# TensorE's order in the first attention written by hand, and identity products ahead of the first weights

## The chip, the cores and the metric

The kernel runs on one core of a Trainium2 chip. The metric is the device time of one execution in microseconds (us), lower is better. A core has a matrix engine (TensorE, "PE" in the profile, with its weight loads as "PEld"), a vector engine (VectorE, "DVE"), an engine for activation functions (ScalarE, "ACT"), a general engine (GpSimd, "POOL") and a sync engine (SyncE, "SP"), which here issues the loads. TensorE writes to PSUM, in banks of 128 x 512 float32; the other engines read it from there. Every engine takes its own instructions strictly in order, and waits for other engines on semaphores.

## What is computed

Two layers over 256 tokens of width 1024, in float32. Layer 0 is a differential attention with 8 heads and a mixer of product-key experts; layer 1 a stick-breaking attention and the same mixer; each sub-layer ends in a layer norm of `alpha * x + f(x)`. The edit touches the first attention:

```python
qkv = x @ w_qkv
q, k, v = qkv[..., :D], qkv[..., D:2 * D], qkv[..., 2 * D:]
q, k = _rope(q), _rope(k)                       # per head of 64
s = einsum('bhmqd,bhmkd->bhmqk', q, k) * scale  # m: two score maps per head
p = softmax(where(mask, s, -inf))
a = p[:, :, 0] - lam * p[:, :, 1]
o = einsum('bhqk,bhkd->bhqd', a, v)
of = o * rsqrt(mean(o * o) + RMS_EPS) * subln_g * (1 - lambda_init)
return of @ w_o
```

The mask is causal in chunks of 64, so the first 128 queries see 128 keys and the second 128 see 256.

## The kernel before

Products with weights are made in three parts. A weight chunk is loaded raw by SyncE; ScalarE copies its upper half to `h` (L144), and VectorE or GpSimd subtracts to get the lower half `l` (L149); `Units.split` alternates the two engines by the parity of `self.n` for units of kind "a". `passes` (L196) then accumulates `xh h`, `xh l` and `xl h`. The raw, `h` and `l` tiles come from a pool of three buffers each. A unit is 128 x 1024.

`diff_attention` (L375) runs in this order of writing:

- The Q projection in eight steps (`moving_steps`, L212), one unit each, four PSUM banks of tag "acc"; `x_in` loads and splits x between the first steps.
- The K projection in eight steps, into the four banks of tag "w". Meanwhile `rope_half` (L386) rotates Q in four pieces, one per token block `b` and half `f` of the columns: VectorE L393, L394 and L395 from PSUM, then an addition on GpSimd (L396). `tr` (L398) transposes the rotated Q on TensorE (L404) in four pairs of 128 columns, and ScalarE (L406) and VectorE (L407) split each into upper and lower half.
- The V projection in eight V steps (`v_steps`, L435) of twelve 512-wide products (L444), with two evacuations (L448) after the fourth and the eighth. K is rotated and transposed as Q was.
- Per group of two heads, `s1(i)`: 64-row score products (L465), b = 1 256 wide and b = 0 128 wide, the mask product (L468), the maximum (VectorE L470), the exponentials (ScalarE L473), the combination of the two maps (L475, L476, L482). `s2(i)`: six transposes (L493) and two ScalarE copies (L494). `s3(i)`: value products (L504, L506), square (ScalarE L516), sum and scaling (VectorE L517 to L520), a power on GpSimd (L521), L522 and L523. `s4(i)`: four transposes (L532) and the split of the attention's output (L533, L534).
- The output projection `wo`, `moving_steps` over eight units (L199), of which the last three go through `tail_passes`; the units of the next projection are loaded and split behind it (`prefetch`, GpSimd L173). Then the layer norm (transposes L312) and the expert mixer's query projection (L244).

PSUM tags "acc" and "w" have four banks each, and scores, transposes and the key projection share "w". A scheduler puts the instructions of each engine in order, by its own estimate of when their inputs are there, except where `tc.manual_schedule` names an engine: there its instructions keep the order in which the code is written. Before, that holds for TensorE in `tail_passes`.

Of the kernel before, what the change touches and what calls it, by code (L numbers as in the profile page):

```python
# [10 lines left out]
F32 = mybir.dt.float32  # L11
# [9 lines left out]
P = 128  # L21
D = 1024
T = 256
NB = 2
# [9 lines left out]
EPS = 1e-5  # L34
GS = 2.0 ** 14
OH = 5

SPANS = []
_o = 0
# [19 lines left out]
def trunk(ctx: ExitStack, tc: tile.TileContext, x, xT, ln_g, ln_b, w_qkv, w_o_a, lam_p, subln, w_kv,  # L59
          w_q, w_o_b, w_pq, sub_k, uT, v, rope, ln_c, out):  # L60
    nc = tc.nc
# [57 lines left out]

    class Units:  # L120
        def __init__(self):
            self.n = 0

        def get_cut(self, src):
            self.n += 1
# [249 lines left out]
    def diff_attention(xh, xl):  # L375
# [19 lines left out]
            nc.vector.tensor_tensor(dv, pv, cs, OP.mult)  # L395
            nc.gpsimd.tensor_tensor(dv, dv, tv, OP.add)  # L396

        def tr(srcv, dstT, tag):  # L398
            for i in range(4):
                pt = psum.tile([P, 2, T], F32, name=tag, tag=tag)  # L400
                for j in range(2):
                    for b in range(NB):
                        n = 2 * i + j
                        nc.tensor.transpose(pt[:, j, b * P:(b + 1) * P], srcv[:, b, n * P:(n + 1) * P], ident)  # L404
                h, l = (t[i] for t in dstT)
                nc.scalar.activation(h, pt, AF.Copy)  # L406
                nc.vector.tensor_tensor(l, pt, h.bitcast(F32), OP.subtract)  # L407
# [6 lines left out]

        halves = [(b, f) for b in range(NB) for f in range(2)]
        aq = accs("acc")
        x_in(0)
        for d, _ in enumerate(moving_steps(aq, xh, xl, src(0), cut=True)):
            if d < 3:
# [3 lines left out]
        ak = accs("w")  # L423
# [110 lines left out]
            nc.vector.scalar_tensor_tensor(ol[:, hs, :], pt, sg, oh[:, hs, :].bitcast(F32), OP.mult, OP.subtract)  # L534

        av = accs("acc")
        for i, _ in enumerate(v_steps(av)):
            if 1 <= i < 5:
                rope_half(ak, KK, *halves[i - 1], 2)
            if i == 4:  # L540
                tr(KK, KT, "w")
                s1(0)
            if i == 5:
                s1(1)
                s2(0)
                s3(0)
            if i == 6:
                s1(2)
                s1(3)
            if i == 7:  # L550
                s2(1)
                s3(1)
        units.later(reg(O_A, NB, D), x)
        oh, ol = xtiles()
        acc = accs("acc")
        wo = moving_steps(acc, oh, ol, lambda d: w_o_a[0, d * P:(d + 1) * P, :], tail=TAIL,
                          ahead=(pq_src(0), range(0, 4096, 1024)))
        for i in range(4):
            if i < 2:
                s2(i + 2)  # L560
                s3(i + 2)
            s4(i, oh, ol)
            next(wo)
            next(wo)
        for _ in wo:
            pass
        return acc
# [516 lines left out]
```

## Time and profile before

| | |
|---|---|
| runs | 1888.84, 1892.78, 1894.35 us |
| median | 1892.78 us |
| profiled execution | 1894.14 us |
| its span, first to last instruction | 1892.3 us |
| TensorE busy | 1831.4 us (97%) |
| granted TensorE clock, mean over the span | 0.989 |

The first attention takes about the first 138 of the 1892 us. TensorE starts at 5.12, the K projection at 31.03, the V projection at 55.63; the next projection's first product stands at 138.22. In a row of the trace the first number is the start, the second the time the instruction took; "x12" says that twelve alike were joined; brackets give the idle time of the engine before it and the engine, tile and line that ended it. Durations of neighbouring products overlap, so the work of a step is read from the starts.

### The profile page before, as it was taken

What the parts mean: (1) busy time and instruction counts of PE and PEld (TensorE: products, weight loads), DVE (VectorE), ACT (ScalarE), POOL (GpSimd) and SP (SyncE); (2) the same over time, 40 slices, a digit from 0 to 9 for tenths busy, and PEclk for the clock granted to TensorE, in tenths of its full rate; (3) what the DMA queues carried; (4) which work ended last, traced back from release to release, by engine and by line L of the source; (5) the groups of instructions that cost most, each with busy time, mean ns of one, the idle gap of its engine ahead of it and who ended that gap; (6) DMA issues with size and microseconds to landing.
All of it is one profiled execution on the core that took longest, in us unless ns stands there. A gap on an engine that the chain in (4) does not pass through costs nothing.

```text
span 1892.3 us, 30931 instructions
## 1 busy us (share of the span) xinstructions
PE 1831.4 (97%) x12264; PEld 1655.8 (87%) x12264; DVE 1232.2 (65%) x2402; ACT 911.5 (48%) x1244; POOL 176.6 (9%) x190
## 2 busy tenths in 40 slices
PE   8999989999999999999999999899999999999997
PEld 6879989898999999978798799889989999998786
DVE  5666988986555555575553569889865555555655
ACT  4545445545444444454447454454544444445442
POOL 5434200000000000000122251000000000000001
PEclk9989999999999999999999999999999999999999
DMA  6533544335555555575643345443355555555753
GB/s 210 177 134 135 184 136 137 123 124 200 179 200 191 191 186 182 186 266 190 211 152 105 123 157 179 133 146 113 134 202 184 191 181 189 185 191 192 255 190 133
DMA packets 90449, 325.40 MB, mean 172 GB/s; under 512 B 10176, under 2 KB 10560, under 8 KB 89664
## 3 DMA queue, kind: packets, MB, share of 16 engines
q1 hardware_dynamic: 90304, 323.43, 50.4%
q8 instruction: 96, 1.57, 0.3%
q14 instruction: 49, 0.40, 0.1%
HBM read 320.24 MB, written 3.15 MB: 171 GB/s over the span
## 4 chain that ended last, share of the span: by engine, by line
PE 77%; DVE 17%; DMA 2%; issue 2%; ACT 1%; POOL 1%; SPq 0%; POOLq 0%; ACTq 0%; DVEq 0%
PE acc L199 38%; PE w L816 28%; PE acc L244 4%; DVE l L149 3%; DVE gl L900 2%; DVE big L873 2%; DVE gh L900 2%; DVE oa L904 1%; PE w L244 1%; PE acc L444 1%; PE w L199 1%; DVE big L707 1%; DVE big L709 1%; DMA big<-in_ln_g 1%; DVE big L714 1%
## 5 line engine op out<-in xcount | busy, mean ns | idle before, releaser
L144 ACT ACTIVATE h<-raw 128x1024 fp32r<-128x1024 f32 x579 | 606.9, 1059 | 854.7 <-PE acc L199 457.0
L149 DVE TENSOR_TENSOR l<-raw,h 128x1024 fp32r<-128x1024 f32 x526 | 642.8, 1235 | 530.4 <-ACT h L144 530.1
L816 PE MATMUL w<-xh,l 128*128 128x256 f32 x2048 | 580.3, 285 | 15.6 <-DVE l L149 15.6
L816 PE MATMUL w<-xh,h 128*128 128x256 f32 x2048 | 586.6, 287 | 2.1 <-ACT h L144 2.1
L816 PE MATMUL w<-xl,h 128*128 128x256 f32 x2048 | 580.6, 284 | 0.0
L816 PEld LDWEIGHTS w<-xh,l 128*128 128x128 f32 x2048 | 392.8, 192 | 21.6 <-DVE l L149 16.6
L199 PE MATMUL acc<-l,wh 128*128 128x512 f32 x1024 | 399.3, 391 | 2.9 <-DVE l L149 2.9
L816 PEld LDWEIGHTS w<-xh,h 128*128 128x128 f32 x2048 | 393.8, 192 | 7.9 <-ACT h L144 2.5
L199 PE MATMUL acc<-h,wl 128*128 128x512 f32 x1024 | 399.5, 391 | 0.0
L816 PEld LDWEIGHTS w<-xl,h 128*128 128x128 f32 x2048 | 393.7, 192 | 4.8
L199 PE MATMUL acc<-h,wh 128*128 128x512 f32 x1024 | 278.3, 391 | 0.0
L199 PEld LDWEIGHTS acc<-l,wh 128*128 128x128 f32 x1024 | 192.6, 188 | 40.0 <-DVE l L149 3.8
L199 PEld LDWEIGHTS acc<-h,wl 128*128 128x128 f32 x1024 | 192.8, 188 | 36.8
L199 PEld LDWEIGHTS acc<-h,wh 128*128 128x128 f32 x1024 | 188.1, 188 | 35.6
L149 POOL TENSOR_TENSOR l<-raw,h 128x1024 fp32r<-128x1024 f32 x53 | 130.4, 2461 | 178.2 <-ACT h L144 167.4
L959 DVE TENSOR_TENSOR wl<-big,wh 128x512 fp32r<-128x512 f32 x128 | 87.0, 687 | 5.1 <-PE acc L199 4.7
L173 POOL TENSOR_TENSOR ahead<-big,ahead 128x512 fp32r<-128x512 f32 x12 | 16.5, 1403 | 754.2 <-ACT ahead L163 754.2
L958 ACT ACTIVATE wh<-big 128x512 fp32r<-128x512 f32 x128 | 78.2, 620 | 12.1 <-PE acc L199 7.8
L915 PE MATMUL acc<-oa,gl 128*128 128x128 f16 x512 | 66.3, 220 | 14.2 <-DVE gl L900 12.7
L295 POOL TENSOR_TENSOR mv<-mv,mhalf 128x1 f32<-128x1 f32 x8 | 4.8, 600 | 745.1 <-DVE mv L294 745.1
L914 PE MATMUL acc<-oa,gh 128*128 128x128 f16 x512 | 70.6, 220 | 0.0
L874 ACT ACTIVATE big<-acc 128x344 f32<-128x344 f32 x128 | 51.4, 453 | 30.5 <-DVE big L873 30.5
(215 smaller groups left out, 1749.2 us busy)
## 6 DMA issues: line engine op xcount, KB each, us to landing
raw<-in_uT SPq DMA_DIRECT2D x256, 512.0 KB, 3.3
raw<-in_v SPq DMA_DIRECT2D x256, 512.0 KB, 3.6
raw<-in_w_qkv SPq DMA_DIRECT2D x23, 512.0 KB, 3.7
raw<-in_w_kv SPq DMA_DIRECT2D x12, 512.0 KB, 4.0
raw<-in_w_o_a SPq DMA_DIRECT2D x8, 512.0 KB, 4.0
big<-in_w_pq SPq DMA_DIRECT2D x8, 512.0 KB, 6.7
raw<-in_w_pq SPq DMA_DIRECT2D x8, 512.0 KB, 5.0
raw<-in_w_q SPq DMA_DIRECT2D x8, 512.0 KB, 3.8
```

Of the source, the lines that this page charges most:

```text
L144: self.h = nc.scalar.activation(h, raw, AF.Copy)
L149: o = e.tensor_tensor(l, raw, h.bitcast(F32), OP.subtract)
L199: nc.tensor.matmul(acc[b][f], a[:, d, ts], w[:, fs], start=(first and q == 0), stop=(last and q == 2))
L244: nc.tensor.matmul(acc[n // 2][:, n % 2, :], w[:, c:c + P], a[:, d, :], start=(d == 0 and q == 0 and n % 2 == 0), stop=(d == DC - 1 and q ...
L816: nc.tensor.matmul(ps[:, k, :], w[:, ds], a[:, d, :], start=(d == 0 and q == 0), stop=(d == DC - 1 and q == 2))
L873: nc.vector.scalar_tensor_tensor(wv[:, 0:N_STORED], pv[:, 0:N_STORED], 1.0 / GS, wv[:, 0:N_STORED], OP.mult, OP.mult)
L874: nc.scalar.activation(wv[:, N_STORED:], pv[:, N_STORED:], AF.Copy, scale=1.0 / GS)
L900: nc.vector.tensor_tensor(dst.rearrange("p r (a b) t -> p r a b t", b=16), hi[:, rs].unsqueeze(3).to_broadcast([P, 4, 8, 16, 2]), lo[:, rs ...
L914: nc.tensor.matmul(ps[:, k, :], gh[:, m, :, e], oa[:, m, :, e], start=True, stop=False)
L915: nc.tensor.matmul(ps[:, k, :], oj[:, m, :, e], oa[:, m, :, e], start=False, stop=True)
L958: nc.scalar.activation(wh, s, AF.Copy)
L959: nc.vector.tensor_tensor(wl, s, wh.bitcast(F32), OP.subtract)
```

## The change

TensorE's part of the first attention, from the first V step to the fourth output step, is put under `tc.manual_schedule`, and the calls are written in another order: the rotations of K all within the first two V steps, the transposes in two pairs, and the stages of one head group between V steps, with `s4(0)`, `s2(3)` and `s4(1)` ahead of the output projection and `s3(2)`, `s3(3)`, `s4(2)`, `s4(3)` between its first steps. The work is the same. Ahead of Q's first product stand 32 products of a 128 x 128 identity in bfloat16 into a "w" bank that nothing reads. `Units.n` starts at 1 in place of 0, which exchanges VectorE and GpSimd in every split of kind "a" of the kernel. From here on line numbers of the changed kernel are higher by 1 up to the rotation and by 4 in the stages (L149 is L150, L396 is L397, L444 is L448, L465 is L469, L493 is L497, L504 is L508, L521 is L525, L532 is L536).

```diff
--- before.py
+++ after.py
@@ -34,6 +34,7 @@
 EPS = 1e-5
 GS = 2.0 ** 14
 OH = 5
+WARM = 32
 
 SPANS = []
 _o = 0
@@ -119,7 +120,7 @@
 
     class Units:
         def __init__(self):
-            self.n = 0
+            self.n = 1
 
         def get_cut(self, src):
             self.n += 1
@@ -395,8 +396,8 @@
             nc.vector.tensor_tensor(dv, pv, cs, OP.mult)
             nc.gpsimd.tensor_tensor(dv, dv, tv, OP.add)
 
-        def tr(srcv, dstT, tag):
-            for i in range(4):
+        def tr(srcv, dstT, tag, pairs=range(4)):
+            for i in pairs:
                 pt = psum.tile([P, 2, T], F32, name=tag, tag=tag)
                 for j in range(2):
                     for b in range(NB):
@@ -414,6 +415,9 @@
 
         halves = [(b, f) for b in range(NB) for f in range(2)]
         aq = accs("acc")
+        warm = psum.tile([P, P], F32, name="w", tag="w")
+        for i in range(WARM):
+            nc.tensor.matmul(warm, identb, identb, start=(i == 0), stop=(i == WARM - 1))
         x_in(0)
         for d, _ in enumerate(moving_steps(aq, xh, xl, src(0), cut=True)):
             if d < 3:
@@ -534,34 +538,42 @@
             nc.vector.scalar_tensor_tensor(ol[:, hs, :], pt, sg, oh[:, hs, :].bitcast(F32), OP.mult, OP.subtract)
 
         av = accs("acc")
+        order_a = ExitStack()
+        order_a.enter_context(tc.manual_schedule(engines={mybir.EngineType.PE}))
+        khalves = [(b, f) for f in range(2) for b in range(NB)]
         for i, _ in enumerate(v_steps(av)):
-            if 1 <= i < 5:
-                rope_half(ak, KK, *halves[i - 1], 2)
+            if i < 2:
+                rope_half(ak, KK, *khalves[2 * i], 2)
+                rope_half(ak, KK, *khalves[2 * i + 1], 2)
+            if i in (1, 3):
+                tr(KK, KT, "w", range(i - 1, i + 1))
+            if i in (2, 3):
+                s1(i - 2)
             if i == 4:
-                tr(KK, KT, "w")
-                s1(0)
-            if i == 5:
-                s1(1)
                 s2(0)
                 s3(0)
+                s1(2)
+            if i == 5:
+                s2(1)
+                s1(3)
             if i == 6:
-                s1(2)
-                s1(3)
-            if i == 7:
-                s2(1)
                 s3(1)
+                s2(2)
         units.later(reg(O_A, NB, D), x)
         oh, ol = xtiles()
+        s4(0, oh, ol)
+        s2(3)
+        s4(1, oh, ol)
         acc = accs("acc")
         wo = moving_steps(acc, oh, ol, lambda d: w_o_a[0, d * P:(d + 1) * P, :], tail=TAIL,
                           ahead=(pq_src(0), range(0, 4096, 1024)))
-        for i in range(4):
-            if i < 2:
-                s2(i + 2)
-                s3(i + 2)
-            s4(i, oh, ol)
+        for i in range(2):
             next(wo)
+            s3(i + 2)
+        for i in range(2):
             next(wo)
+            s4(i + 2, oh, ol)
+        order_a.close()
         for _ in wo:
             pass
         return acc
```

What this does to the order of instructions is shown at three places. The first is GpSimd around the rotation of K. `l<-raw,h` is the lower half of a unit, `big<-big` the addition of a rotation; `l_513`, `l_557` and `l_681` belong to the second, fourth and sixth V step before; `l_530`, `l_596` and `l_748` to the first, third and fifth after. Before:

```order
L149 TENSOR_TENSOR l_513<-raw_510,h_512 128x1024
L396 TENSOR_TENSOR big_70<-big_70 128x512 x3
L149 TENSOR_TENSOR l_557<-raw_554,h_556 128x1024
L396 TENSOR_TENSOR big_70<-big_70 128x512
L149 TENSOR_TENSOR l_681<-raw_678,h_680 128x1024
L149 TENSOR_TENSOR l_892<-raw_889,h_891 128x1024
```

After:

```order
L150 TENSOR_TENSOR l_530<-raw_527,h_529 128x1024
L397 TENSOR_TENSOR big_70<-big_70 128x512
L150 TENSOR_TENSOR l_596<-raw_593,h_595 128x1024
L397 TENSOR_TENSOR big_70<-big_70 128x512 x3
L150 TENSOR_TENSOR l_748<-raw_745,h_747 128x1024
L150 TENSOR_TENSOR l_919<-raw_916,h_918 128x1024
```

Three additions stood together ahead of the next split; now one addition, then the split of the third V step, then the other three.

The second place is TensorE around the start of the output projection, `L199` before and `L200` after. Before, with `L504`/`L506` the value products, `L532` the output's transposes, `L493` the transposes of the probabilities:

```order
L504 MATMUL om<-big 128x128
L506 MATMUL om<-big 128x128 x2
L532 MATMUL w<-ident,big 128x128 x4
L493 MATMUL w<-ident,big 128x128 x6
L199 MATMUL acc<-h,xh 128x512
L199 MATMUL acc<-l,xh 128x512
L199 MATMUL acc<-h,xh 128x512
L199 MATMUL acc<-l,xh 128x512
L199 MATMUL acc<-h,xh 128x512
L199 MATMUL acc<-l,xh 128x512
```

After, with the last V step (`L448`) ahead:

```order
L448 MATMUL acc<-h,xh 128x512
L448 MATMUL acc<-l,xh 128x512
L448 MATMUL acc<-h,xl 128x512
L536 MATMUL w<-ident,big 128x128 x4
L497 MATMUL w<-ident,big 128x128 x6
L536 MATMUL w<-ident,big 128x128 x4
L200 MATMUL acc<-h,xh 128x512
L200 MATMUL acc<-l,xh 128x512
L200 MATMUL acc<-h,xl 128x512
L200 MATMUL acc<-h,xh 128x512
```

Two groups of output transposes now stand before the first output product, with one group of probability transposes between them; before, one group stood there and the other transposes followed among the output steps.

The third place is GpSimd at the end of the attention, where `big<-big,mhalf` is the power of `s3` and `ahead` a lower half for the next projection. Before:

```order
L663 MEMSET big_70 128x16
L521 TENSOR_TENSOR big_70<-big_70,mhalf_88 128x2x2 x3
L149 TENSOR_TENSOR l_1062<-raw_1059,h_1061 128x1024
L173 TENSOR_TENSOR ahead_1135<-big_70,ahead_1131 128x512
L173 TENSOR_TENSOR ahead_1136<-big_70,ahead_1132 128x512
L173 TENSOR_TENSOR ahead_1143<-big_70,ahead_1139 128x512
L173 TENSOR_TENSOR ahead_1144<-big_70,ahead_1140 128x512
```

After:

```order
L675 MEMSET big_70 128x16
L525 TENSOR_TENSOR big_70<-big_70,mhalf_88 128x2x2
L150 TENSOR_TENSOR l_1079<-raw_1076,h_1078 128x1024
L525 TENSOR_TENSOR big_70<-big_70,mhalf_88 128x2x2
L150 TENSOR_TENSOR l_1130<-raw_1127,h_1129 128x1024
L525 TENSOR_TENSOR big_70<-big_70,mhalf_88 128x2x2
L174 TENSOR_TENSOR ahead_1171<-big_70,ahead_1167 128x512
L174 TENSOR_TENSOR ahead_1172<-big_70,ahead_1168 128x512
```

Three powers stood together ahead of one split of an output unit; now a split stands behind the second power and another behind the third.

## Rows read from the trace of the kernel before

**Rows 1.** the page, part 1: engine, busy us, share, instructions.

```profile
PE 1831.4 (97%) x12264; PEld 1655.8 (87%) x12264; DVE 1232.2 (65%) x2402; ACT 911.5 (48%) x1244; POOL 176.6 (9%) x190
```

**Rows 2.** stretches: length, busy us of PE, PEld, DVE, ACT, POOL, granted clock, DMA.

```profile
84.92:107.61 22.69, 21.50 (x115) 19.27 (x115) 14.48 (x41) 13.40 (x51) 4.22 (x50) 0.62 0.15 47
...
55.63:138.22 82.59, 78.34 (x425) 65.36 (x424) 54.83 (x109) 45.38 (x110) 33.22 (x68) 0.90 0.40 142
```

**Rows 3.** groups, 55.6 to 140: busy us, mean ns; idle us before, by releaser.

```profile
L144 ACT ACTIVATE h<-raw 128x1024 fp32r<-128x1024 f32 x14 | 14.9, 1063 | 15.8 <-PE acc L199 8.3 <-PE acc L444 4.0 <-PE w L199 1.7
...
L199 PE MATMUL acc<-h,xh 128*128 128x512 f32 x32 | 12.5, 397 | 0.6 <-ACT xh L533 0.6
...
L199 PE MATMUL acc<-h,xl 128*128 128x512 f32 x32 | 11.9, 397 | 0.4 <-DVE xl L534 0.4
...
L473 ACT ACTIVATE big<-w,big 128x256 f32<-128x256 f32 x16 | 7.4, 470 | 3.7 <-DVE big L470 3.7
...
L521 POOL TENSOR_TENSOR big<-big,mhalf 128x4 f32<-128x4 f32 x4 | 4.1, 1015 | 18.3 <-DVE big L520 18.3
...
L518 DVE TENSOR_REDUCE big<-big 128x4 f32<-128x512 f32 x4 | 2.8, 688 | 2.3 <-ACT big L516 2.3
...
L312 PE MATMUL w<-ident,big 128*128 128x128 f32 x16 | 2.5, 290 | 2.2 <-ACT big L303 1.1 <-DVE big L322 1.1
...
L448 ACT ACTIVATE big<-acc 128x512 f32<-128x512 f32 x4 | 2.3, 607 | 1.4 <-PE acc L444 1.3
```

**Rows 4.** TensorE, 33 to 88: start, us, what it is, idle before.

```profile
33.75 1.07 PE L199 MATMUL w<-h,xh 128*128 128x512 f32 x4
...
36.48 1.08 PE L199 MATMUL w<-h,xh 128*128 128x512 f32 x4
...
71.10 0.98 PE L465 MATMUL w<-qk 64*128 64x256 f32 x12
...
85.94 0.97 PE L465 MATMUL w<-qk 64*128 64x256 f32 x6 [1.02 <-ACT big L473]
...
87.00 1.55 PE L465 MATMUL w<-qk 64*128 64x256 f32 x6
```

**Rows 5.** TensorE, the kernel's first 14 us.

```profile
5.12 2.29 PE L199 MATMUL acc<-h,xh 128*128 128x512 f32 x4 [5.12 <-ACT h L132]
...
8.06 0.63 PE L199 MATMUL acc<-l,xh 128*128 128x512 f32 x1
...
9.02 0.40 PE L199 MATMUL acc<-h,xl 128*128 128x512 f32 x1
...
10.06 1.19 PE L199 MATMUL acc<-h,xh 128*128 128x512 f32 x4 [0.19 <-ACT h L144]
12.52 0.50 PE L199 MATMUL acc<-l,xh 128*128 128x512 f32 x1 [1.26 <-POOL l L149]
```

**Rows 6.** VectorE, 54 to 85.

```profile
54.47 0.42 DVE L393 TENSOR_TENSOR big<-w,big 128x256 f32<-128x256 f32 x1 [1.71 <-PE w L199]
...
55.74 0.41 DVE L393 TENSOR_TENSOR big<-w,big 128x256 f32<-128x256 f32 x1
...
69.86 1.23 DVE L149 TENSOR_TENSOR l<-raw,h 128x1024 fp32r<-128x1024 f32 x1 [3.83 <-ACT h L144]
...
81.05 1.40 DVE L482 SCALAR_TENSOR_TENSOR big<-big 128x128 f32<-128x128 f32 x4
82.49 2.22 DVE L517 TENSOR_TENSOR big<-big 128x4 f32<-128x4 f32 x1
```

**Rows 7.** GpSimd, 54 to 85.

```profile
54.25 2.41 POOL L149 TENSOR_TENSOR l<-raw,h 128x1024 fp32r<-128x1024 f32 x1 [3.71 <-ACT h L144]
56.61 3.81 POOL L396 TENSOR_TENSOR big<-big 128x512 f32<-128x512 f32 x3
60.36 3.39 POOL L149 TENSOR_TENSOR l<-raw,h 128x1024 fp32r<-128x1024 f32 x1
...
82.14 2.56 POOL L149 TENSOR_TENSOR l<-raw,h 128x1024 fp32r<-128x1024 f32 x1 [8.04 <-DVE big L482]
```

## The prediction

> **What bounds the kernel now.** The page's first part comes first: TensorE is busy 97% of the span and nothing else comes near it [rows 1]. What an edit outside TensorE brings is therefore only what it takes from TensorE's waits, from its clock, or from the length of its products. The table by stretches comes second. From the first V product at 55.63 to the first product of the next projection at 138.22 there are 82.59 us, and the granted clock averages 0.90. All of that loss lies in 84.92 to 107.61, which ran at 0.62 [rows 2]. With levels of 1.0 and 0.5 that is (1 - 0.62) x 22.69 / 0.5 = 17.2 us at 1.2 GHz, the lower level. The groups by line are third: they give TensorE's waits of the stretch, 1.02 for the banks of the scores [rows 4], 0.6 and 0.4 for the output projection's operands, and 2.2 in the layer norm [rows 3]. The two layer norm waits are outside the edit. So the stretch holds at most 2.0 us of removable waits and the clock's loss. The rest is products.
>
> **The change, part by part.**
>
> *Old waits removed:* 1.02 + 0.6 + 0.4 = 2.0 us [rows 3, 4].
>
> *The long stretch at the lower clock goes.* It began about 1 us after the wait that ended at 85.94, and held through score products, transposes and value products in a row. All eight V steps were over by then. In the new order every group of such small products has a V or output step of twelve 512-wide products behind it. What the lower clock cost: six serial 256-wide scores took 0.97 us at 85.94 and 1.55 at 87.00 [rows 4], so 37% of the time there; at worst half of it. Of 17.2 us that is 6.4 to 8.6. I take 7.0, near the row.
>
> *Scores written alternately.* Twelve 256-wide score products that alternate between two tiles took 0.98 us, and six that fill one tile took 0.97 [rows 4], so alternating halves them. Before, two of four groups ran serially in their wide part, and one in its narrow part. At full clock that is 2 x 0.96, and about 0.4 for the narrow one (an estimate): 2.3 us saved. The written order alternates throughout.
>
> *New waits.* TensorE now takes its work in a fixed order, so each group waits for its own chain while ready products stand behind it. A V or output step is 36.48 - 33.75 = 2.73 us of TensorE [rows 4]. I count from the first V product. VectorE and GpSimd do not run two-input operations on on-chip data at the same time: a VectorE operation on four elements took 2.22 us, ending with GpSimd's split of 82.14, and the split of 60.36 took 3.39 instead of 2.41 us [rows 6, 7]. I use that below.
>
> A, the first key transposes, behind two V steps, so wanted at 5.45. Units that start at the other parity put the second V step's low half on VectorE, 1.23 us, from about 54.25 [rows 6, 7], to -0.15. Then come the rotations, 55.74 - 54.47 = 1.27 each [rows 6], still in the old order (first token block, both halves, then the second), so that a pair of transposes needs three of them. GpSimd's first addition (1.27, a third of 3.81 [rows 7]) ends at 2.4. Its queue then has the next split, 2.41, to 4.8, the second addition to 6.1, then VectorE's waiting split of 1.23 goes ahead to 7.3, and the third addition ends at 8.6. The wait is 3.1. Without the exclusion it is 1.9. Queued behind it are TensorE's third V step and everything later.
>
> B, the second head group, which needs banks freed by ScalarE. Its queue has the eight exponentials of the group before, then two evacuations of 0.61, an upper half of 1.06, two copies of about 0.6 and the two exponentials of 0.47 that free the group's own banks [rows 3]: 1.2 + 1.06 + 1.2 + 0.94 = 4.4. TensorE has 1.0 of work against it, so 3.4. Before it stands about 0.5 for the last exponential. Behind it stands about 1.2, since VectorE's key copy is queued behind a small operation that waits for GpSimd's split as at 82.49. Sum 5.0; without the last part 3.8, and with half of the rest hidden 2.
>
> C, the first value products, right behind their transposes: two copies of 0.6, with an upper half of 1.06 ahead of them in ScalarE's queue [rows 3]. Bounds 0.6 and 2.3; I take 1.4. D, the fourth score group: 0.5 for one exponential, 0 to 1.
>
> E, the transposes of the second group's output, now written ahead of all output steps. From the end of its value products the chain is: ScalarE's exponentials and a queued upper half, 1.5, the square 0.6; VectorE held by a lower half until about 3.4 after the products; a reduction of 0.69; small operations 0.5; the power on GpSimd, 1.02; behind it in the same queue a split of 2.41, which shuts out the next small VectorE operation; then that and a 0.69 multiplication [rows 3, 7]. That gives 3.4 + 0.69 + 0.5 + 1.02 + 2.41 + 0.9 = 8.9. TensorE has a V step, two groups of six transposes and one of four against it, some 4.6, so the wait is 4.3. Without the exclusion it is 1.9.
>
> A to E: 3.1 + 5.0 + 1.4 + 0.5 + 4.3 = 14.3 us, where the chains without the exclusion give 14.3 - 1.2 - 1.2 - 2.4 = 9.5.
>
> A rule of the Trainium skill speaks further against this order. Rows show such blocking for two-input operations with both inputs on chip; for the four multiply-adds of a group (1.40 us [rows 6]) no row has them beside GpSimd. "SBUF — State Buffer", section "Who interferes with whom", has any VectorE instruction with two SBUF inputs contend with a GpSimd instruction that reads SBUF. By that rule these four would be held as well, and the sum would be some 0.7 us higher (an estimate from half of the row); the sum goes without it.
>
> *New drops of the clock.* At the start, where TensorE had been idle until 5.12, its first eight products took 0.63 each, and 0.40 once the clock had risen [rows 5]: 8 x 0.23 = 1.8 us for one drop that dense products follow. Waits of 1.1 us in the layer norm [rows 3] cost no clock: the stretch from 107.61 on ran at 1.00. A, B and E are three times as long or more. None to four such drops, or one as long as before, gives 0 to 7. I take two, 3.6 us.
>
> *The start.* Thirty-two identity products before the first weights cost nothing while the first chunk's twelve products still end before the second chunk's upper half, which arrives at 10.06 whatever TensorE does [rows 5]. If they ran on past 5.12 by more than that slack, each would show in full. Parity moves the second chunk's low half to VectorE, so the 1.26 us wait at 12.52 [rows 5] goes. The third chunk's low half moves to GpSimd instead, which takes 2.41 - 1.23 = 1.2 longer [rows 6, 7], and I count 0.8 of that. So -0.5, with bounds -1.3 and +0.8.
>
> *Everything later.* The parity of all alternating splits flips, in the output projection and in layer 1 too. Each moves 1.2 us to or from a place where it mostly hides behind a step of 2.73. I count 0, with 1.2 either way.
>
> **Sum.** -2.0 - 7.0 - 2.3 + 14.3 + 3.6 - 0.5 = +6.1 us on the profiled execution of 1894.14 (1892.3 of span and 1.84 around it): 1900.2. That execution lies 1.4 above the median of the runs, so for a median I give 1899. A difference under 0.3%, 5.7 us, can't be told from no change. Without new waits the gains are 11.8 us, so the change is faster beyond measure if new waits and drops stay under 6.1, and slower if they pass 17.5. My 17.9 is just past that.
>
> **Rivals.**
>
> *The written order does what it says.* The chains A to E end before TensorE arrives, because the rotations, exponentials and splits run earlier when nothing on TensorE holds their inputs back. Then only about 2 us of waits stay, and 2.0 + 7.0 + 2.3 + 0.5 - 2 = 9.8 us are gained: 1883. It decides if A and E both vanish and B falls to 2, which takes another order on GpSimd than the one built, since its split stands between the additions. For it speaks that VectorE and ScalarE are busy only 54.83 and 45.38 of 82.59 us [rows 2], so that there is room. Chance 0.17, faster.
>
> *The waits come, smaller or without drops.* Either the exclusion rarely falls on a chain (waits 9.5, one drop of 1.8: -0.5, so 1892), or the waits are 14.3 and the clock holds as it did in the layer norm (+2.5, so 1895). For the second speaks that dense products follow each wait. Chance 0.28, within 0.3%.
>
> *One long stretch at the lower clock comes back.* Before, a wait of 1.02 us among 64-row scores was followed by one; here waits B and C lie among scores too. Then drops cost 7.0 in place of 3.6: 1894.14 + 9.5 - 1.4, or 1902. "TensorE: Matmul & The Clock Gate", section "HAM oscillation — how this bites in real kernels", describes this: bursts of matmuls with waits between them fall to the lower clock again each time. The trace agrees at 85.94 and disagrees at the layer norm, which keeps the chance at 0.15, slower.
>
> **How the numbers follow.** The forecast has 0.38: waits of 12 to 16 and drops of 2 to 5 give 1895 to 1902, 0.28 of it slower by over 0.3% and 0.10 within it. With the rivals: faster 0.17, within 0.3% 0.38, slower 0.43; the 0.02 that is left, a gain that no case names, I put on faster. The range reaches from 1888 to 1905. Below it lies the first rival, above it the long stretch with the upper bounds of the waits.
>
> **What would show it.** Right for A: a TensorE wait of about 3 us before the first key transposes, released by GpSimd's addition. For E: 4 us before the last transposes ahead of the output steps, released by VectorE, with GpSimd's split running until just before. For B: several waits released by ScalarE in the second scores. The granted clock from 84.92 on at 1.00 except for short dips, and score groups of twelve at 0.98. Wrong if the total of TensorE's waits between the first V product and the layer norm is under 8 us, if one dip lasts over 10 us, or if the first projection's end moves by more than 1 us.

## The result

The changed kernel takes 1899.38 us (median of nine runs, 1896.43 to 1904.43) and the kernel before 1890.77 (nine runs, 1887.06 to 1894.35). The ratio is 1.0053, 95% interval 1.004 to 1.0065: slower by half a per cent, and 1.0 lies outside the interval. The profiled execution took 1903.33 us, with a span of 1901.6, against 1894.14 and 1892.3 before.

TensorE's busy time is the same as in [rows 1], 1831.5 us against 1831.4; the span is 9.3 us longer. Part 1 of the page after:

```profile
PE 1831.5 (96%) x12296; PEld 1654.6 (87%) x12296; DVE 1235.5 (65%) x2403; ACT 911.1 (48%) x1244; POOL 171.5 (9%) x189
```

The stretch from the first V product to the end of the output projection, before and after (length, busy us of PE, PEld, DVE, ACT and POOL, granted clock, DMA share, GB/s):

```profile
55.63:133.75 78.12, 76.09 (x409) 63.70 (x407) 51.36 (x100) 43.73 (x109) 32.66 (x67) 0.89 0.43 150
```

```profile
53.93:140.69 86.76, 73.05 (x409) 59.91 (x407) 54.35 (x102) 42.80 (x109) 32.59 (x67) 0.88 0.40 142
```

The products themselves became 3.0 us cheaper (76.09 to 73.05), and the stretch 8.6 us longer. The difference between length and busy time is TensorE's waiting: 2.0 us before, 13.7 after. Busy time counts a product for as long as it takes, so at the lower clock it counts for more. TensorE's timeline of the changed kernel has it in these rows (start, duration, what it is, idle before and its releaser):

```profile
30.29 1.07 PE L200 MATMUL w<-h,xh 128*128 128x512 f32 x4
...
53.93 0.39 PE L448 MATMUL acc<-h,xh 128*128 128x512 f32 x1
...
63.25 1.76 PE L405 MATMUL w<-ident,big 128*128 128x128 f32 x7 [3.61 <-POOL big L397]
...
69.55 0.98 PE L469 MATMUL w<-qk 64*128 64x256 f32 x12
...
76.05 0.97 PE L469 MATMUL w<-qk 64*128 64x256 f32 x11 [0.25 <-ACT big L477]
...
79.85 0.47 PE L469 MATMUL w<-qk 64*128 64x128 f32 x1 [2.62 <-ACT big L477]
81.01 1.54 PE L469 MATMUL w<-qk 64*128 64x128 f32 x11 [0.68 <-DVE qk L408]
...
89.14 0.49 PE L508 MATMUL om<-big 128*128 128x128 f32 x2 [1.30 <-ACT big L498]
...
112.80 1.09 PE L536 MATMUL w<-ident,big 128*128 128x128 f32 x4 [5.22 <-DVE big L527]
```

The waits stand at four of the prediction's five places: A before 63.25, B at 76.05 to 81.01, C before 89.14 and E before 112.80. D is missing. At A, B and E the clock fell, at C (1.30 us) it did not. The table by stretches, in pieces of 2 us (same columns):

```profile
60.00:62.00 2.00, 0.00 (x0) 0.00 (x0) 2.00 (x1) 0.63 (x1) 2.00 (x2) 1.00 0.48 98
62.00:64.00 2.00, 0.75 (x4) 0.75 (x5) 0.08 (x1) 0.00 (x0) 2.00 (x2) 0.52 0.78 213
64.00:66.00 2.00, 2.00 (x8) 1.80 (x7) 1.02 (x2) 1.20 (x2) 2.00 (x2) 0.50 0.56 213
...
80.00:82.00 2.00, 1.32 (x11) 1.13 (x11) 1.55 (x3) 0.71 (x4) 0.33 (x1) 0.50 0.32 68
...
112.00:114.00 2.00, 1.20 (x5) 1.24 (x6) 1.31 (x2) 0.08 (x1) 0.00 (x0) 0.50 0.52 168
...
144.00:146.00 2.00, 1.95 (x9) 1.92 (x10) 1.51 (x4) 0.56 (x1) 0.00 (x0) 0.50 0.15 61
```

In this profile the clock falls to the lower level, 1.2 GHz, each time while TensorE still waits, and stays there into the dense products behind the wait: 64.66 to 68.9 in the third V step, whose products start 0.43 us apart and not 0.23. The last row is a fourth fall, in the layer norm, where the kernel before kept its clock in its first profile.

### The profile page after: what moved, and what is told of

It reads as the page before. It is cut to its first block, busy times and chain, and to the rows that moved or that the text cites. A ratio compares the mean times of both kernels' runs of the same rounds, so it can differ in the third digit from the quotient of the medians.

```text
span 1901.6 us, 30990 instructions
## 1 busy us (share of the span) xinstructions
PE 1831.5 (96%) x12296; PEld 1654.6 (87%) x12296; DVE 1235.5 (65%) x2403; ACT 911.1 (48%) x1244; POOL 171.5 (9%) x189
## 4 chain that ended last, share of the span: by engine, by line
PE 73%; DVE 18%; DMA 3%; issue 2%; ACT 2%; POOL 2%; SPq 0%; ACTq 0%; POOLq 0%; DVEq 0%
PE acc L200 37%; PE w L828 28%; DVE l L150 4%; PE acc L245 4%; DVE gl L912 2%; DVE big L885 2%; DVE gh L912 2%; DMA raw<-in_w_qkv 2%; DVE oa L916 1%; PE w L245 1%; ACT h L145 1%; DVE big L719 1%; DVE big L721 1%; DVE big L726 1%; DMA raw<-in_v 1%
## 5 line engine op out<-in xcount | busy, mean ns | idle before, releaser
L150 DVE TENSOR_TENSOR l<-raw,h 128x1024 fp32r<-128x1024 f32 x527 | 642.5, 1232 | 526.3 <-ACT h L145 526.3
L200 PE MATMUL acc<-l,wh 128*128 128x512 f32 x1024 | 398.9, 391 | 3.1 <-DVE l L150 3.1
L200 PE MATMUL acc<-h,wl 128*128 128x512 f32 x1024 | 399.1, 391 | 0.0
L200 PE MATMUL acc<-h,wh 128*128 128x512 f32 x1024 | 278.4, 391 | 0.0
L200 PEld LDWEIGHTS acc<-l,wh 128*128 128x128 f32 x1024 | 192.5, 188 | 40.3 <-DVE l L150 4.0
L200 PEld LDWEIGHTS acc<-h,wl 128*128 128x128 f32 x1024 | 192.7, 188 | 36.9
L200 PEld LDWEIGHTS acc<-h,wh 128*128 128x128 f32 x1024 | 187.9, 188 | 36.0 <-ACT h L145 0.6
L150 POOL TENSOR_TENSOR l<-raw,h 128x1024 fp32r<-128x1024 f32 x52 | 125.4, 2412 | 177.7 <-ACT h L145 172.7
L970 ACT ACTIVATE wh<-big 128x512 fp32r<-128x512 f32 x128 | 78.1, 619 | 11.2 <-PE acc L200 6.9
```

Of the source, the lines that this page charges most:

```text
L150: o = e.tensor_tensor(l, raw, h.bitcast(F32), OP.subtract)
L200: nc.tensor.matmul(acc[b][f], a[:, d, ts], w[:, fs], start=(first and q == 0), stop=(last and q == 2))
L970: nc.scalar.activation(wh, s, AF.Copy)
```

## The experiments

Every kernel was run with the kernel before on the same chip, whose median over all those runs was 1889.8 to 1890.8. In the table, "stretch" is the time from the first V product to the end of the output projection, "waits" TensorE's idle time in it, "lower clock" the time in it at half clock; these come from one profiled execution each. The profiled executions lie up to 4.0 us from their kernel's median, single runs up to 7.5. The rest of the kernel, from the next projection's first product on, took 1751.6 to 1757.4 us in these profiles, so a difference of a few us in the stretch need not show in the whole. The ratio is taken over all runs and not from the two medians; the two ways differ by up to 1.4 us, and both are given where that matters.

| kernel | median us | ratio to before (95%) | stretch | waits | lower clock |
|---|---|---|---|---|---|
| before, first profile | 1890.8 | | 78.1 | 2.0 | 17.1 |
| before, second profile | | | 73.1 | 2.9 | 3.4 |
| changed, first profile | 1899.38 | 1.0053 (1.004 to 1.0065) | 86.8 | 13.7 | 20.5 |
| changed, second profile | | | 85.8 | 12.8 | 17.1 |
| identity products alone | 1889.76 | 0.9999 (0.9989 to 1.0009) | 76.6 | 1.7 | 13.7 |
| exchange of engines alone | 1896.49 | 1.0037 (1.0026 to 1.0049) | 82.8 | 4.8 | 20.5 |
| written order alone | 1891.99 | 1.0010 (1.0 to 1.0019) | 76.6 | 7.5 | 6.8 |
| changed, without the exchange | 1893.70 | 1.0012 (1.0001 to 1.0024) | 77.8 | 7.5 | 10.2 |
| changed, rotation in written order | 1898.18 | 1.0044 (1.0027 to 1.0061) | 82.3 | 11.9 | 10.2 |
| changed, waits filled | 1897.45 | 1.0035 (1.0021 to 1.0049) | 81.7 | 6.3 | 6.8 |
| changed, output units on VectorE | 1896.58 | 1.0029 (1.0016 to 1.0043) | 84.8 | 11.6 | 17.1 |
| stages moved apart | 1891.16 | 1.0005 (0.9995 to 1.0014) | 75.6 | 7.8 | 6.8 |
| the same, second chunk on VectorE | 1891.66 | 1.0008 (0.9997 to 1.0019) | 75.8 | 8.0 | 6.8 |
| stages further apart | 1886.88 | 0.9992 (0.9979 to 1.0004) | 72.0 | 3.8 | 3.4 |

### The three parts of the change, one by one

**Identity products alone**

```diff
+        warm = psum.tile([P, P], F32, name="w", tag="w")
+        for i in range(WARM):
+            nc.tensor.matmul(warm, identb, identb, start=(i == 0), stop=(i == WARM - 1))
         x_in(0)
```

> The kernel before with only the 32 identity products ahead of the first projection. My theory: the first eight products take 0.40 us apart-time instead of 0.63, but the second chunk's upper half still arrives at about 10 us and the 1.26 us wait for GpSimd's lower half stays, so the K projection starts within 0.5 us of 31.03 and the whole stays within 0.3% of before. Rival (the clock raised early is what moved the V projection's start from 55.63 to 53.93): the K projection starts 0.7 us or more earlier, and the whole gains 1 to 2 us.

The K projection started at 31.32, against 31.03 and 31.18 in the two profiles of before, and the ratio is 0.9999. TensorE's timeline of this kernel shows why:

```profile
1.53 3.59 PE L420 MATMUL w<-identb 128*128 128x128 bf16 x32 [1.53 <-DVE identb L89]
...
7.86 0.39 PE L200 MATMUL acc<-l,xh 128*128 128x512 f32 x1
...
9.93 1.19 PE L200 MATMUL acc<-h,xh 128*128 128x512 f32 x4 [1.00 <-ACT h L145]
12.38 0.51 PE L200 MATMUL acc<-l,xh 128*128 128x512 f32 x1 [1.26 <-POOL l L150]
```

The product at 7.86 takes 0.39 us, where [rows 5] still has 0.63 at 8.06, but the second chunk arrives at 9.93, as at 10.06 in [rows 5], and TensorE waits 1.00 us for it and again 1.26 for its lower half. The products cost nothing and bring nothing that the interval, 0.1% either way, would show.

**The exchange of engines alone**

```diff
-            self.n = 0
+            self.n = 1
```

> The kernel before with only the counter of units starting at 1, so that VectorE and GpSimd exchange every alternating split. Theory one (the exchange is what makes the waits of 3.6 and 5.2 us in the changed kernel, because a GpSimd split then stands between the rotation's additions and behind a power): the start gains about 1.2 us, but waits come up in the first attention released by GpSimd's additions and by VectorE's L522, and the whole is 1 to 5 us slower than before. Theory two (the written order makes them, whichever engine splits): only the start's gain is left, 1 us faster, and no new wait over 1 us.

It costs 7.0 us by the ratio and 5.8 by the medians, more than the 1 to 5 expected. The K projection starts at 30.44, so the start's gain of some 0.7 us is there. The waits are not the expected ones: with the order left to the scheduler they lie among scores and output steps, and most are released by ScalarE. The first of them, behind its exponentials:

```profile
83.87 0.66 PE L493 MATMUL w<-ident,big 128*128 128x128 f32 x4 [1.51 <-ACT big L473]
84.78 0.44 PE L493 MATMUL w<-ident,big 128*128 128x128 f32 x2 [0.26 <-ACT big L473]
85.48 0.97 PE L465 MATMUL w<-qk 64*128 64x256 f32 x6 [0.26 <-ACT big L473]
```

Theory one named the right edit and a wrong mechanism. With the order left to the scheduler, the exchange also moves groups on TensorE: the narrow scores of the first group stand at 73.94, right behind the wide ones at 72.81, where before they stood at 76.86 and 71.10. The waits of 4.8 us in place of 2.0 and 2.9 are not the whole cost. Over its seven runs the granted clock averages 0.9879, over 28 runs of the kernel before 0.9905, some 10 us more at the lower clock; at the 43% found below that is 4 us (an estimate).

**The written order alone, and the change without the exchange**

```diff
-            self.n = 1
+            self.n = 0
...
-        warm = psum.tile([P, P], F32, name="w", tag="w")
...
```

> The changed kernel without the identity products and with the counter at 0 as before: the written order alone. Theory one (the exchange of engines makes the waits before the first key transposes, 3.6 us, and before the second output transposes, 5.2 us): both shrink under 0.5 us, two or three waits of 1.0 to 1.5 us stay among the scores and value products, the granted clock falls in fewer places, the 17 us at half clock of before are gone, and the time is 3 to 8 us under before. Theory two (a fixed order of TensorE makes them by itself): both stay above 2.5 us and the time stays 5 to 10 us above before.

> The changed kernel with the counter at 0, identity products kept. By theory one it is as the written order alone to within 1 us, so 3 to 8 us under before; if the identity products carry the start's gain it is 1 to 2 us under the written order alone. By theory two it stays 5 to 10 us above before.

The edit shown is the written order alone; the change without the exchange has only its line of the counter, and keeps the identity products. Both are 0.1% slower than before, neither 3 to 8 us faster nor 5 to 10 slower. Of the two waits that theory one gave to the exchange, the first is gone: no wait before the key transposes. The second halved. TensorE's timeline of the written order alone:

```profile
74.69 0.58 PE L466 MATMUL w<-qk 64*128 64x128 f32 x5 [3.15 <-ACT big L474]
...
82.28 0.49 PE L505 MATMUL om<-big 128*128 128x128 f32 x2 [1.30 <-ACT big L495]
...
103.63 1.09 PE L533 MATMUL w<-ident,big 128*128 128x128 f32 x4 [2.53 <-DVE big L524]
```

So theory one holds for A and for half of E, theory two for B and C. By the ratios the written order alone costs 1.9 us, the exchange alone 7.0, and both with the identity products 10.0: the edits roughly add up, and the exchange is most of it. That they add up does not make the mechanism the same: the exchange alone has other waits than the exchange within the written order.

### The waits of the written order

**A: rotation in written order**

```diff
...
+            if roped:
+                queue_after(r, roped[-1])
...
+            roped.append(nc.vector.tensor_tensor(dv, pv, cs, OP.mult))
```

> The changed kernel with one edit: VectorE is made to rotate K in the order in which the calls are written, the first half of the columns for both token blocks first, so that the first key transposes need two of GpSimd's additions and not three. If step A of the prediction is right (GpSimd's third addition ends the wait, behind a split of 2.41 us and VectorE's split): the wait before the first key transposes falls from 3.6 to about 1.2 us, and the granted clock does not fall there, which gives back up to 2.6 us more; part of the 2.4 us comes back as longer waits among the scores. Together 2 to 5 us under the changed kernel's 1899.4. If the wait has another cause (bank or projection), it stays at 3 us or more.

GpSimd and VectorE of the changed kernel show the chain of A as it was laid out, addition, split, and three additions with VectorE's split between:

```profile
56.11 1.30 POOL L397 TENSOR_TENSOR big<-big 128x512 f32<-128x512 f32 x1 [2.43 <-DVE big L396]
57.36 2.41 POOL L150 TENSOR_TENSOR l<-raw,h 128x1024 fp32r<-128x1024 f32 x1
59.73 4.70 POOL L397 TENSOR_TENSOR big<-big 128x512 f32<-128x512 f32 x3
```

```profile
59.73 2.35 DVE L150 TENSOR_TENSOR l<-raw,h 128x1024 fp32r<-128x1024 f32 x1
```

Three additions take 3.81 alone [rows 7], and 4.70 here; the split takes 1.23 alone [rows 6], and 2.35 here. With two additions needed in place of three, the wait falls from 3.61 to 1.60 us, where about 1.2 was expected:

```profile
61.26 0.98 PE L409 MATMUL w<-ident,big 128*128 128x128 f32 x7 [1.60 <-POOL big L401]
```

No fall of the clock is left at that place, and the stretch is 3.5 to 4.5 us shorter. Of that the medians show only 1.2 us and the ratios 1.7, from four runs with intervals that overlap, where 2 to 5 were expected; the step is shown by the rows, its worth in time is not settled by these runs.

**E: output units on VectorE**

```diff
-        wo = moving_steps(acc, oh, ol, lambda d: w_o_a[0, d * P:(d + 1) * P, :], tail=TAIL,
+        wo = moving_steps(acc, oh, ol, lambda d: w_o_a[0, d * P:(d + 1) * P, :], "v", TAIL,
```

> The changed kernel with one edit: the output projection's units are all split on VectorE, so that GpSimd's split no longer stands behind the power of the second group. If step E is right that this split (2.34 us) shuts out the next small VectorE operation: that operation takes 0.16 us in place of 2.29, the wait before the second output transposes falls from 5.2 to about 3 us, and the time by 2 us or a little more under 1899.4. If the wait is the chain's own length, it stays over 4.5 us.

In the changed kernel the small operation behind the power (L526) starts after GpSimd's split and ends with it (GpSimd first, VectorE second):

```profile
108.51 1.02 POOL L525 TENSOR_TENSOR big<-big,mhalf 128x4 f32<-128x4 f32 x1 [6.28 <-DVE big L524]
109.50 2.34 POOL L150 TENSOR_TENSOR l<-raw,h 128x1024 fp32r<-128x1024 f32 x1
```

```profile
109.57 2.29 DVE L526 TENSOR_TENSOR big<-big 128x4 f32<-128x4 f32 x1 [1.14 <-POOL big L525]
111.96 0.69 DVE L527 TENSOR_TENSOR big<-om,big 128x512 f32<-128x512 f32 x1
```

With that split gone from GpSimd, VectorE and TensorE, each in its own timeline:

```profile
108.22 0.16 DVE L526 TENSOR_TENSOR big<-big 128x4 f32<-128x4 f32 x1
```

```profile
109.79 1.09 PE L536 MATMUL w<-ident,big 128*128 128x128 f32 x4 [3.23 <-DVE big L527]
```

0.16 for 2.29 us, a wait of 3.23 for 5.22, and 2.8 us off the median (4.5 by the ratios, whose intervals just overlap). The exclusion, that the small operation on VectorE is held while GpSimd's split runs, is worth 2.0 us of TensorE's wait here, near the 2.4 of the prediction.

### The clock

**Waits filled with products that nothing reads**

```diff
+        def keep(dst, n):
+            for k in range(n):
+                nc.tensor.matmul(dst, identb, identb, start=(k == 0), stop=(k == n - 1), skip_group_check=True)
...
+                if tag == "w" and i == 0:
+                    keep(pt[:, 0, 0:P], 48)
...
+            if i == 1:
+                keep(pt[:, 0, 0:P], 80)
```

> The changed kernel with identity products that nothing reads ahead of the first key transposes (48 of them) and of the second output transposes (80), so that TensorE is busy through most of the two longest waits; they are sized to end before the waits do, at 0.056 us each. If the waits bring the granted clock down and that costs some 2.6 and 2.1 us behind them: the clock stays at 1.00 through both places, the waits themselves end when they did, and the time is 4 to 5 us under the changed kernel's 1899.4. If the lower clock behind the waits costs nothing, since the work there waits for something else anyway, the time stays within 1 us of 1899.4.

TensorE's timeline around both places, and the clock there:

```profile
60.51 2.85 PE L401 MATMUL w<-identb 128*128 128x128 bf16 x48
...
64.30 0.87 PE L411 MATMUL w<-ident,big 128*128 128x128 f32 x6 [0.81 <-POOL big L397]
...
105.42 4.63 PE L401 MATMUL w<-identb 128*128 128x128 bf16 x80
110.66 0.66 PE L544 MATMUL w<-ident,big 128*128 128x128 f32 x4 [0.61 <-DVE big L533]
```

```profile
62.00:64.00 2.00, 1.48 (x26) 1.29 (x23) 1.12 (x1) 0.00 (x0) 2.00 (x2) 1.00 0.70 241
64.00:66.00 2.00, 1.70 (x11) 1.58 (x12) 0.49 (x1) 1.09 (x2) 2.00 (x3) 1.00 0.80 223
...
112.00:114.00 2.00, 2.00 (x11) 1.63 (x10) 0.75 (x1) 0.04 (x1) 0.00 (x0) 1.00 0.23 90
```

TensorE works without useful work, the products end before the transposes can start (waits of 0.81 and 0.61 us are left), and the clock stays at 2.4 GHz in both places. The stretch is 4 to 5 us shorter than in the two profiles of the changed kernel. The 4 to 5 us were expected of the whole, which is 1.9 us faster by the medians and 3.4 by the ratios, with intervals that overlap. The granted clock speaks for the 3.4: it averages 0.9914 over these eight runs and 0.9892 over nine of the changed kernel, some 8 us less at the lower clock, which at 43% is 3.6 us (an estimate). In this profile 1.1 us of the stretch's gain were lost ahead of it, where the clock fell from 12 to 15 us, behind a wait of 1.76 us for the second chunk.

**Both kernels profiled again**

> The kernel before, unchanged, profiled a second time. Its first profiled execution lies 3.4 us above the median of its runs. If that excess is in the first attention (a stretch at half clock that is longer in some executions), the second profile has the next projection's first product earlier than 138.22 and a shorter stretch at half clock. If the excess lies elsewhere, both are as in the first.

> The changed kernel, unchanged, profiled a second time. The waits of 3.6, 3.6, 1.3 and 5.2 us are set by the order of the engines and should repeat to 0.2 us; the dips of the clock behind them may fall elsewhere or be missing, which would account for its runs lying between 1896 and 1904.

The kernel before had its long stretch at the lower clock in one of its two profiles only. The same wait of 1.02 us stands among the same scores, until 85.04, and the clock holds. It falls at 95.2, within a wait of 0.85 us that the first profile does not have, for 3.4 us in all. The stretches, and TensorE's row at the second wait:

```profile
86.00:88.00 2.00, 2.00 (x17) 1.80 (x17) 1.53 (x4) 1.48 (x9) 0.00 (x0) 1.00 0.75 260
88.00:90.00 2.00, 2.00 (x22) 1.70 (x21) 1.93 (x7) 1.50 (x5) 0.00 (x0) 1.00 0.21 78
...
94.00:96.00 2.00, 1.15 (x9) 0.94 (x8) 1.97 (x6) 1.55 (x8) 0.71 (x15) 0.79 0.00 0
96.00:98.00 2.00, 2.00 (x11) 2.00 (x10) 1.16 (x5) 1.50 (x6) 1.72 (x36) 0.50 0.05 12
```

```profile
95.42 1.51 PE L493 MATMUL w<-ident,big 128*128 128x128 f32 x6 [0.85 <-ACT big L494]
```

TensorE's busy time in the stretch is 70.25 there and 76.09 in the first profile, so 13.7 us at the lower clock cost 5.8, or 43%. The span is 5.2 us shorter, all of it in the first attention (the next projection starts at 132.37, not 138.22).

Over 28 runs of the kernel before the granted clock averages 0.9905; the first profile has 0.989, the second 0.992. So neither profile is the usual execution. In these runs the time goes with the clock: 1.3 us more for each 0.001 less.

The changed kernel had its waits at the same places: 2.64, then 0.26, 2.61 and 0.83, then 1.30 and 5.16 us, with the clock low at the same three places and again in the layer norm, from 143.6 to 147.0. Only A did not repeat to 0.2 us. The 1.0 us between the two profiles comes from VectorE's split ahead of the rotation: in the first it started at 52.55 beside a GpSimd split and took 2.21 us, in the second 1.23.

### A better order

**Stages moved apart, with the counter at 0**

```diff
-            if i in (1, 3):
-                tr(KK, KT, "w", range(i - 1, i + 1))
-            if i in (2, 3):
-                s1(i - 2)
...
+        tr(KK, KT, "w", range(0, 2))
+        next(units_v)
+        next(units_v)
+        s1(0)
+        tr(KK, KT, "w", range(2, 4))
+        next(units_v)
+        s1(1)
+        s2(0)
+        next(units_v)
+        s3(0)
+        s1(2)
+        next(units_v)
+        s2(1)
+        s1(3)
...
```

> The written order with the counter at 0, identity products kept, and the stages moved apart: the second V step, first key transposes, two V steps, first scores and the other key transposes, a V step, then one score group, one group of transposes or one of value products each between V steps. By the chains of ScalarE, VectorE and GpSimd as the traces have them no wait but those of the layer norm passes 0.8 us. If waits and the clock drops behind them are all that the written order costs: granted clock 1.00 from the first V step to the output projection, first scores in pairs throughout, and 4 to 8 us under the kernel before. If small products keep the clock low by themselves whatever waits there are, it stays within 2 us of the kernel before.

> The version with the stages moved apart, and the lower half of the second chunk of the Q projection on VectorE in place of GpSimd, all other splits as before. The wait of 1.26 us at 12.5 goes; if the next chunk follows on VectorE without a new wait, the Q and K projections end 1.2 us earlier and the whole is about 1 us under the version without that edit; if the x chunks on VectorE collide with it, nothing is gained.

Both missed. B is gone (waits of 0.75 and 0.25 are left, in two places), but 1.67 and 0.52 us stand before the third transposes of probabilities, and 3.40 before the second output transposes. The clock fell at 99.25, behind the first two of these waits and ahead of the last, and stayed low for 6.8 us. The ratio is 1.0005, and 1.0008 with the second chunk on VectorE: there the K projection starts 1.25 us earlier, and nothing of it is left in the time.

**Stages further apart**

```diff
         s2(3)
-        s4(1, oh, ol)
...
         next(wo)
         s3(2)
+        s4(1, oh, ol)
```

Against the version before, this moves `s4(1)`; here also all output units are split on VectorE, so the two edits are not told apart.

> The version with the stages moved apart, with two edits: the output transposes of the second head group stand behind the first output step and the third group's value products in place of ahead of all output steps, and all eight output units are split on VectorE, so that no GpSimd split stands behind a power. In the version without them a wait of 3.4 us stood there, released by VectorE's multiplication, and the clock fell behind it. If distance is what the chain of square, sums, power and multiplication needs: no wait over 1.5 us there, no half clock behind it, and 4 to 6 us under the version without these edits, which makes it 0.2 to 0.3% under the kernel before. If the wait only moves to the first output step (its operands come from the same chains), it gains under 2 us.

The stretch, with the columns as above:

```profile
54.82:126.86 72.04, 68.18 (x409) 55.21 (x407) 50.14 (x102) 43.00 (x109) 27.68 (x65) 0.98 0.46 163
```

No single wait passes 0.75 us, they add up to 3.8, and the stretch is the shortest of all. The clock fell even so, at 99.5 for 3.4 us, behind waits of 0.61, 0.52 and 0.41 us among small groups:

```profile
100.00:102.00 2.00, 2.00 (x6) 1.54 (x6) 0.86 (x2) 0.00 (x0) 0.93 (x1) 0.50 0.75 285
```

That no half clock would stand there was missed, and a rival stays open: that groups of small products with short gaps bring the clock down, without a long wait. The median is 4.3 us under that of the version without these edits, within the 4 to 6 expected, but by the ratios it is 2.5. Against before it is 2.9 under by the medians and 1.5 by the ratio, short of the 0.2 to 0.3% expected; its interval, 0.9979 to 1.0004, does not exclude no change. It beats the changed kernel clearly, and the kernel before not beyond doubt.

## Why the prediction came out right, and where it was off

The forecast was 1899, slower. Its mechanism, waits that a fixed order puts in place of the scheduler's gaps, is what the rows show. Step by step:

- **A**, put at 3.1: 3.61 and 2.64 in the two profiles, released by GpSimd's addition, and by the chain that was laid out. The first is longer because VectorE's split ahead of the chain was itself held, which the prediction had free at 1.23 us.
- **B**, put at 5.0: 0.25 + 2.62 + 0.68 = 3.55. The part with ScalarE's queue was put at 3.4 and took 2.6, and the last exponential 0.25 and the key copy 0.68, where 0.5 and 1.2 were put.
- **C**, put at 1.4: 1.30. **D**, put at 0.5: none. **E**, put at 4.3: 5.22. Together 14.3 forecast, 13.7 measured.
- **Scores**, put at -2.3: the 256-wide groups of twelve take 0.97 to 0.99 us throughout. By the busy times, with 43% of the time at the lower clock taken off, before has 70.25 - 1.5 = 68.8 and the version with the stages further apart 68.18 - 1.5 = 66.7: 2.1.
- **The old lower clock**, put at -7.0: 17.1 us cost 7.3 in the execution that the sum was made against. The step that failed is to take that execution for the usual one. In the second it would have been 1.5 (3.4 x 0.43).
- **New drops**, put at two of 1.8, 3.6 together: the term that was mis-sized. There were three in the stretch, each long enough to outlast the wait, and one in the layer norm. By the busy time the three cost 73.05 - 66.7 = 6.3, and the fourth 0.5 up to the next projection's first product and 0.8 in the 24 us behind it. That is 7.6, twice the forecast. The price was taken from the start, where eight products ran at the lower clock (by their starts, 0.43 and 0.23 us apart, 0.20 each and not 0.23); behind A alone there were seven transposes and nine 512-wide products.
- **The start**, put at -0.5: the K projection began at 30.29, 0.7 earlier, since the wait of 1.26 us is gone and 0.48 stands at the third chunk, where 0.8 was counted. The V projection began at 53.93, 1.7 earlier than in the first profile and 0.8 than in the second; the difference is mostly a wait before the query transposes, which only the first profile of before has and no term named:

```profile
38.77 0.87 PE L404 MATMUL acc<-ident,big 128*128 128x128 f32 x6 [0.78 <-POOL big L396]
```

- **Everything later**, put at 0: from the next projection's first product to the end 1755.9 us, and 1754.1 before, of which 0.8 is the clock's tail just named.

For the profiled pair the sum with the measured terms is -2.0 - 7.3 - 2.1 + 13.7 + 7.6 - 1.7 = +8.2, and the first product of the expert mixer stands 8.3 us later (169.6 against 161.3). The forecast of +6.1 was 2 to 3 us low against this pair. The median of before was lower over more runs than the one it was laid on (1890.8, not 1892.8). These two errors cancel, and by that luck 1899 met the median to half a microsecond; the change by medians is 8.6 us, where 6.2 was forecast. What it had wrong is the clock. Old and new drops together were booked at -7.0 + 3.6 = -3.4 us. Over its nine runs the changed kernel's granted clock averages 0.9892, that of the kernel before 0.9905 to 0.9913 in its three sets of 18 to 28 runs. So the change spends some 5 to 8 us more at the lower clock, not less, which at 43% costs 2 to 3 us (an estimate). The slowdown is that of the waits, and the clock adds to it instead of taking from it.

The prediction's rule of the Trainium skill on VectorE and GpSimd ("SBUF — State Buffer", section "Who interferes with whom") was kept out of the sum for want of a row. There is one now, in the changed kernel without the exchange of engines (VectorE, then GpSimd):

```profile
96.62 3.56 DVE L486 SCALAR_TENSOR_TENSOR big<-big 128x128 f32<-128x128 f32 x4
```

```profile
97.17 2.72 POOL L150 TENSOR_TENSOR l<-raw,h 128x1024 fp32r<-128x1024 f32 x1 [4.12 <-issue]
```

Four multiply-adds that took 1.40 us [rows 6] took 3.56 beside a split. The trace agrees with the rule: these are held too. In this place VectorE loses 2.2 us, more than the 0.7 that was named; TensorE's wait for them is 0.21 us there (100.23), and what the delay adds to later waits no run separates.

Of the rivals, the one in which the written order does what it says did not come, since the split stood between the additions as the order of instructions had shown. The rival with one long stretch at the lower clock came in another form, several short ones. What the Trainium skill says in "TensorE: Matmul & The Clock Gate", section "HAM oscillation — how this bites in real kernels", that matmuls in bursts with waits between them fall back to the lower clock each time, agrees with both profiles at A, B and E, and not at C, where 1.30 us brought no fall.

What stays open: why one program spends 17.1 us at the lower clock in one execution, from just behind a wait of 1.02 us, and holds its clock behind the same wait in another; what beside the length of a wait decides, as 1.60 us at A brought no fall and gaps of 0.4 to 0.6 us did; how much of A's worth in the stretch reaches the median; and whether the order with the stages further apart is truly faster than the kernel before.

## What to carry to other kernels

An order that is written out for one engine fixes where it waits: lay out, for each small group in it, the queue of every other engine that feeds it, and put as much dense work between a group and its producers as their chain is long. Count the engine whose turn a parity or a rotation sets as part of the order, since a one-character edit here cost 6 to 7 us, more than the rewritten order did. And profile the kernel before twice where its clock falls, before a gain is booked on it.

## What was not expected of the hardware

In both profiles of the changed kernel the granted clock fell to 1.2 GHz at or just behind each wait of 2.6 to 5.2 us and rose again 3 to 8 us after that wait; in the first profile that cost 6.3 us of TensorE's time in three places. Products that nothing reads, at 0.058 to 0.059 us each, held the clock at 2.4 GHz through waits of the same length. A short wait is no safeguard: in the last version the clock fell behind three of 0.4 to 0.6 us. Two executions of the same program differed by 13.7 us at the lower clock and by 5.8 us of TensorE's time.
